# Two passes instead of three for the gate and up products of small experts

## The chip, the cores and the metric

The kernel runs on one NeuronCore of a Trainium2 chip. The metric is the device time of one execution in microseconds (us): the kernel before takes 2128.33 us, the median of three runs (2125.3 to 2130.84). Engines are named as in the profile: PE is TensorE (PEld its weight loads), DVE is VectorE, ACT is ScalarE, POOL is GpSimd and SP is the queue that issues loads.

## What is computed

Two transformer blocks on 512 tokens of width 1024, in float32. The part that matters here is the mixture of experts that ends the first block: 64 experts of hidden width 256, of which each token takes 8. Cut to this, the reference is:

```
out = swiglu(h_pad[tok], w_gu[e], w_down[e])      # silu(x @ gate) * (x @ up) @ down, for each expert e
acc = acc.at[tok].add(out * wts[:, None])         # its tokens only, weighted
```

`w_gu` is 1024 x 512 for each expert (gate and up side by side), `w_down` is 256 x 1024, so an expert has 3 MB of weights.

## The kernel before, in words

Products that have to keep float32 accuracy are made of three passes. Each operand is split into a high part (`hi`, rounded to the format `R` that PE takes in one pass) and a low part (`lo`, the rest): ACT writes `hi` by a copy, DVE writes `lo` by a subtraction. `mm3` (line 142) then adds high times high, high times low and low times high in PSUM.

The expert stage is the loop in `experts` (line 1256). Experts are ordered by how many tokens chose them, and the table `CAPS` gives each place in this order a fixed room: 3 experts with room for 192 tokens, 6 for 128, 21 for 96, 24 for 64 and 8 for 32, beside 2 fixed ones with 128. `plan` (line 1149) makes groups of them: two experts of 64 share one block of 128 rows (12 groups), a 96 and a 32 share one (8 groups), the other 13 experts of 96 and all of 128 have a block each, and an expert of 192 has a block of 128 and one of 64. This gives 44 groups, 47 blocks and 67 pairs of an expert and a block. The kinds of groups are mixed evenly over the stage.

For each block the rows are gathered by an indirect DMA (`xg`), turned by PE and split (`expert_rows`: tiles `xT`, tokens along the 128 columns that PE holds still). For each expert, its weights come in three loads of 1 MB (`raw`; gate and up two, down one), each split in two pieces (`split_unit`, lines 132 and 133: `whi` by ACT, `wlo` by DVE, 128 x 1024 each). `expert_in` (line 998) multiplies: the token block stands still, 512 columns of weights move past it, 8 steps of 128 along the width of 1024, three passes each, so 24 matmuls for each pair of an expert and a block, whatever the expert's room. `act` is silu of gate (ACT, line 1011) times up (DVE, line 1012). One group later `act` is turned and split (`expert_turn`), `expert_out` multiplies by down (12 matmuls), ACT scales the result into `ey`, and the result is added to the tokens in two ways: the first 384 columns by a product with a 0/1 matrix into PSUM (`expert_parts`, `expert_add`: tiles `eoh`, `eys`, `acc`), the others by an indirect DMA that adds in HBM (`expert_send`, tile `cb`, issued by POOL).

Each engine works through its own list in order. The lists are made by a scheduler when the program is built, from the order of the code and its own estimate of times; buffers decide the rest: five `raw` tiles, eight pieces of `whi` and `wlo` each, four PSUM tiles `mm`. A load is issued when DVE has split the tile that it overwrites. Behind the loop a branch (line 1312) skips a loop for experts with more tokens than their room.

Of the kernel before, what the change touches and what calls it, by code (L numbers as in the profile page):

```python
# [21 lines left out]
T = 512  # L22
# [43 lines left out]
class Kernel:  # L66
# [918 lines left out]
    def expert_rows(self, tiles, pp, xg, m=128):  # L985

        nc = self.nc
        pool, tags = tiles
        xT = [pool.tile([128, KD, 128], R, tag=tag, name="xT", bufs=2)[:, :, 0:m] for tag in tags]
        for u in range(2):  # L990
            p2 = pp.tile([128, 4, 128], F, tag="mm", name="tp", bufs=4)[:, :, 0:m]
            for k in range(4):
                c = (4 * u + k) * 128
                nc.tensor.transpose(p2[:, k], xg[0:m, c:c + 128], self.ident[0:m, 0:m])
            self.split_ps(xT[0][:, 4 * u:4 * u + 4], xT[1][:, 4 * u:4 * u + 4], p2)
        return xT

    def expert_in(self, pp, gu, blocks, between=None):

        nc = self.nc  # L1000
        pss = [pp.tile([128, 512], F, tag="mm", name="mm", bufs=4) for _ in blocks]
        for u in range(2):
            w = self.split_unit(gu[u].rearrange("p (k n) -> p k n", k=4), 4, 512)
            for ps, (xT, *_) in zip(pss, blocks):
                for k in range(4):
                    kk = 4 * u + k
                    self.mm3(ps[0:xT[0].shape[2]], [z[:, kk] for z in xT], [z[:, k] for z in w], kk == 0, kk == KD - 1)
            if u == 0 and between:
                between()
        for ps, (xT, a, p0, p1) in zip(pss, blocks):  # L1010
            nc.scalar.activation(a[p0:p1], ps[p0:p1, 0:256], AF.Silu)
            nc.vector.tensor_mul(a[p0:p1], a[p0:p1], ps[p0:p1, 256:512])  # L1012

    def expert_turn(self, mp, pp, a):

# [27 lines left out]
    def expert_parts(self, mp, y, row, bufs=2):  # L1043

        nc = self.nc
        m = row.shape[0]
        yh, yl = (mp.tile([128, CA], R, tag=f"eys{i}", name="eys", bufs=bufs)[0:m] for i in range(2))
        nc.scalar.activation(yh, y[0:m, :CA], AF.Copy)  # L1048
        last = nc.gpsimd.tensor_sub(yl, y[0:m, :CA], yh.bitcast(F))  # L1049
        oh = mp.tile([128, T], R, tag="eoh", name="eoh", bufs=bufs)[0:m]  # L1050
# [119 lines left out]
    def experts(self, mp, pp, h2d, cb, acc, shared, gT, sums, grow, ahead, extra):  # L1170
# [42 lines left out]
        def turn(g):  # L1213

            if g < len(groups):
                xT[g] = []
                for b in groups[g][1]:
                    free.append(xg_of[count[1]])
                    xT[g].append(self.expert_rows(tiles, pp, free[-1], b[-1][2]))
# [23 lines left out]
        sums()  # L1243
        n = len(xgs)
        more = grow()
        tiles = more, ("xT0", "xT1")
        room(mp, AHEAD2)
        free.extend(xgs[n:])
        for _ in range(AHEAD2):
# [6 lines left out]
        for g in range(len(groups) + 1):  # L1256
# [36 lines left out]
            if g < len(groups):  # L1293
                es, bs = groups[g]
                a = [mp.tile([128, 256], F, tag="eact", name="act", bufs=4)[0:b[-1][2]] for b in bs]
                now = g, a, []
                for j, e in enumerate(es):
                    e = number(e)
                    now[2].append(e)
                    self.expert_in(pp, gu(e), [(xT[g][b], a[b], p0, p1) for b, parts in enumerate(bs)  # L1300
                                               for i, p0, p1, _ in parts if i == j], None if j else advance)
                    finish()
            else:
                advance()
# [4 lines left out]
        ahead()  # L1309
        xp = extra.enter_context(tc.tile_pool(name="extra", bufs=1))  # L1310
        total = self.further(xp)
        with tc.If(total > 0):
            cnt = xp.tile([128, 1], F, name="xcnt")
            nc.vector.memset(cnt, 0.0)
            with tc.For_i(0, total):
                pos, aux, e = self.extra_block(xp, cnt)
                row, wt, gi, _ = self.slot_tables(xp, pp, [[(pos, aux, 0, 128, 0)]])[0]
                ev = nc.sync.value_load(e[0:1, 0:1], min_val=0, max_val=63)
                self.gather(gi, xgs[0], h2d)
                a = mp.tile([128, 256], F, tag="eact", name="act", bufs=4)  # L1320
                self.expert_in(pp, gu(ev), [(self.expert_rows(tiles, pp, xgs[0]), a, 0, 128)])
                y = mp.tile([128, D], F, tag="ey", name="ey", bufs=2)
                self.expert_out(pp, dn(ev), [(self.expert_turn(more, pp, a), wt, y, 0, 128)])
                self.expert_add(acc, *self.expert_parts(xp, y, row, 1)[0])
# [635 lines left out]
```

## Time and profile before

| what | value |
|---|---|
| median of three runs | 2128.33 us |
| the profiled execution: its own time | 2128.15 us |
| the profiled execution: span from first to last instruction | 2126.4 us |
| PE busy over the span | 2038.1 us (96%) |
| DVE busy over the span | 1425.5 us (67%) |
| ACT busy over the span | 1090.8 us (51%) |
| POOL busy over the span | 486.2 us (23%) |
| moved by DMA | 386.68 MB, mean 182 GB/s |

The shares are means over stages that differ. The expert stage, from the first gate product at 585.7 us to the last down product at 1282.7 us, is a third of the span; its own rows stand in the section below. A busy time in a row of a window counts a moment once, however many instructions overlap in it; a group's mean is the length of one instruction, which on DVE and PE can overlap the next.

### The profile page before, as it was taken

What the parts mean: (1) busy time and instruction counts of PE and PEld (TensorE: products, weight loads), DVE (VectorE), ACT (ScalarE), POOL (GpSimd) and SP (SyncE); (2) the same over time, 40 slices, a digit from 0 to 9 for tenths busy, and PEclk for the clock granted to TensorE, in tenths of its full rate; (3) what the DMA queues carried; (4) which work ended last, traced back from release to release, by engine and by line L of the source; (5) the groups of instructions that cost most, each with busy time, mean ns of one, the idle gap of its engine ahead of it and who ended that gap; (6) DMA issues with size and microseconds to landing.
All of it is one profiled execution on the core that took longest, in us unless ns stands there. A gap on an engine that the chain in (4) does not pass through costs nothing. (4 is left out here: it accounts for less than half of the span.)

```text
span 2126.4 us, 28083 instructions
## 1 busy us (share of the span) xinstructions
PE 2038.1 (96%) x10311; PEld 1663.4 (78%) x10311; DVE 1425.5 (67%) x2444; ACT 1090.8 (51%) x1569; POOL 486.2 (23%) x307
## 2 busy tenths in 40 slices
PE   7999999999899999999999996999999999999998
PEld 4777888877787788877887784877788878888886
DVE  6667767647899799989999785455853345333344
ACT  7445443233387788878887884334232224232232
POOL 0322231011144343524334213011100001010110
PEclk9999999999899999999999998999999999999999
DMA  7211136633499899999999885312122333222221
GB/s 297 70 41 48 53 111 261 235 110 147 177 322 335 290 341 352 339 325 307 337 336 337 289 290 188 132 60 70 50 89 79 114 115 116 92 100 99 99 80 40
DMA packets 69713, 386.68 MB, mean 182 GB/s; under 512 B 11374, under 2 KB 12351, under 8 KB 30020
## 3 DMA queue, kind: packets, MB, share of 16 engines
q1 hardware_dynamic: 56932, 357.56, 45.6%
q0 software_dynamic: 12640, 27.29, 5.5%
q8 instruction: 82, 1.34, 0.2%
q14 instruction: 59, 0.48, 0.1%
HBM read 369.99 MB, written 23.55 MB: 185 GB/s over the span
## 5 line engine op out<-in xcount | busy, mean ns | idle before, releaser
L133 DVE TENSOR_TENSOR wlo<-raw,whi 128x1024 fp32r<-128x1024 f32 x586 | 728.0, 1258 | 252.0 <-ACT whi L132 244.0
L132 ACT ACTIVATE whi<-raw 128x1024 fp32r<-128x1024 f32 x592 | 621.0, 1057 | 385.6 <-PE mm L147 190.7
L146 PE MATMUL mm<-whi,xT 128*128 128x512 f32 (+2 forms) x536 | 219.7, 410 | 0.1
L147 PE MATMUL mm<-wlo,xT 128*128 128x512 f32 (+2 forms) x536 | 211.9, 395 | 0.0
L148 PE MATMUL mm<-whi,xT 128*128 128x512 f32 (+2 forms) x536 | 211.9, 395 | 0.0
L1039 POOL DMA_INDIRECT cb<-ey,sgi x67 | 130.9, 1954 | 233.4 <-ACT ey L1035 148.4
L146 PE MATMUL mm<-hT,whi 128*128 128x512 f32 x320 | 127.0, 397 | 0.0
L147 PE MATMUL mm<-hT,whi 128*128 128x512 f32 x320 | 125.8, 394 | 0.0
L148 PE MATMUL mm<-hT,wlo 128*128 128x512 f32 x320 | 125.5, 392 | 0.0
L147 PE MATMUL mm<-x,whi 128*128 128x512 f32 x304 | 122.5, 403 | 0.0
L148 PE MATMUL mm<-x,wlo 128*128 128x512 f32 x304 | 120.8, 398 | 0.0
L146 PE MATMUL mm<-x,whi 128*128 128x512 f32 x304 | 120.8, 397 | 0.0
L148 PEld LDWEIGHTS mm<-whi,xT 128*128 128x128 f32 (+2 forms) x536 | 96.8, 181 | 27.8
L146 PEld LDWEIGHTS mm<-whi,xT 128*128 128x128 f32 (+2 forms) x536 | 97.2, 181 | 23.1 <-DVE act L1012 0.5
L1565 POOL TENSOR_TENSOR relu<-relu 128x512 f32<-128x512 f32 x32 | 42.9, 1341 | 315.0 <-ACT relu L1563 315.0
L147 PEld LDWEIGHTS mm<-wlo,xT 128*128 128x128 f32 (+2 forms) x536 | 97.2, 181 | 22.3
L1049 POOL TENSOR_TENSOR eys<-ey,eys 128x384 fp32r<-128x384 f32 (+2 forms) x47 | 79.2, 1686 | 141.2 <-ACT eys L1048 114.3
L148 PE MATMUL mm<-whi,eaT 128*128 128x512 f32 (+2 forms) x268 | 105.8, 396 | 0.4 <-DVE eaT L153 0.2
L147 PE MATMUL mm<-wlo,eaT 128*128 128x512 f32 (+2 forms) x268 | 105.8, 395 | 0.0
L146 PE MATMUL mm<-whi,eaT 128*128 128x512 f32 (+2 forms) x268 | 105.8, 395 | 0.0
L146 PE MATMUL mm<-y,whi 128*128 128x512 f32 (+2 forms) x272 | 103.2, 380 | 0.0
L148 PE MATMUL mm<-y,wlo 128*128 128x512 f32 (+2 forms) x272 | 103.1, 379 | 0.0
(534 smaller groups left out, 4488.9 us busy)
## 6 DMA issues: line engine op xcount, KB each, us to landing
raw<-in_w_expert_gu SPq DMA_DIRECT2D x128, 1024.0 KB
raw<-in_w_expert_down SPq DMA_DIRECT2D x64, 1024.0 KB
raw<-in_w_in SPq DMA_DIRECT2D x41, 1024.0 KB
raw<-in_w_ff SPq DMA_DIRECT2D x32, 1024.0 KB
raw<-in_w_ada SPq DMA_DIRECT2D x24, 1024.0 KB
raw<-in_w_out SPq DMA_DIRECT2D x8, 1024.0 KB
raw<-in_w_v SPq DMA_DIRECT2D x4, 1024.0 KB
raw<-in_w_ret_up SPq DMA_DIRECT2D x4, 1024.0 KB
```

Source lines behind the costliest of these rows:

```text
L132: nc.scalar.activation(hi, rv[:, k:k + n], AF.Copy)
L133: (engine or nc.vector).tensor_sub(lo, rv[:, k:k + n], hi.bitcast(F))
L146: mm(ps, ah, bh, start=start, stop=False)
L147: mm(ps, ah, bl, start=False, stop=False)
L148: mm(ps, al, bh, start=False, stop=stop)
L1039: self.nc.gpsimd.indirect_dma_start(out=cb, out_offset=bass.IndirectOffsetOnAxis(ap=gi, axis=0), in_=y[p0:p1, CA:], in_offset=None, bounds ...
L1049: last = nc.gpsimd.tensor_sub(yl, y[0:m, :CA], yh.bitcast(F))
L1565: nc.gpsimd.tensor_mul(sq, r, r)
```

## The change

For an expert with room for up to 64 tokens the high and the low part of its rows are put side by side in the 128 columns that PE holds still. One pass over `whi` and one over `wlo` then give both parts' products: rows 0 to n of PSUM hold the high part's, rows n to 2n the low part's (n tokens). Their sum is the result; it holds low times low too, which three passes leave out. So 16 matmuls take the place of 24 for each such pair of an expert and a block. In exchange ACT copies the second half of the rows out of PSUM (`esum`, n x 512), DVE adds the first half to it, and silu and product then read `esum` from SBUF. The pairs concerned are the 24 experts of 64, the 8 of 32 and the second blocks of the 3 experts of 192: 35 of 67.

`expert_rows` writes the parts where they are wanted: for two experts of 64 in one block by one copy and one subtraction of the same size as before with other strides, for a 96 beside a 32 by two of each (96 and 32 tokens wide). The tile `xT` holds both parts in one tile of the size of the two before. Apart from this, `add()` moves ahead of the branch, and the loop behind it uses other buffers; the trace shows no instruction of that loop.

```
     def expert_in(self, mp, pp, gu, blocks, between=None):
...
+                    if len(xT) == 2:
+                        self.mm3(ps[0:xT[0].shape[2]], [z[:, kk] for z in xT], [z[:, k] for z in w],
+                                 kk == 0, kk == KD - 1)
+                    else:
+                        for i, z in enumerate(w):
+                            nc.tensor.matmul(ps[0:xT[0].shape[2]], xT[0][:, kk], z[:, k],
+                                             start=kk == i == 0, stop=kk == KD - 1 and i == 1)
...
+            if len(xT) == 2:
+                nc.scalar.activation(a[p0:p1], ps[p0:p1, 0:256], AF.Silu)
+                nc.vector.tensor_mul(a[p0:p1], a[p0:p1], ps[p0:p1, 256:512])
+            else:
+                n = p1 - p0
+                s = mp.tile([128, 512], F, tag="esum", name="esum", bufs=2)[p0:p1]
+                nc.scalar.activation(s, ps[n:2 * n], AF.Copy)
+                nc.vector.tensor_add(s, ps[0:n], s)
+                nc.scalar.activation(a[p0:p1], s[:, 0:256], AF.Silu)
+                nc.vector.tensor_mul(a[p0:p1], a[p0:p1], s[:, 256:512])
...
     def expert_rows(self, tiles, pp, xg, parts=((0, 128),)):
...
+            elif w == 64:
+                v = x.rearrange("p k (j h w) -> p k h j w", j=2, h=2)
+                cut = [(lambda z: z.rearrange("p k (j w) -> p k j w", j=2), v[:, :, 0], v[:, :, 1])]
+                out = [(x[:, :, 0:128],), (x[:, :, 128:256],)]
+            else:
+                cut = [(lambda z: z[:, :, 0:w], x[:, :, 0:w], x[:, :, 256 - w:256]),
+                       (lambda z: z[:, :, w:m], x[:, :, w:m], x[:, :, m:256 - w])]
+                out = [(x[:, :, 0:w], x[:, :, 256 - w:256]), (x[:, :, w:256 - w],)]
...
+            for some, hi, lo in cut:
+                self.split_ps(hi[:, 4 * u:4 * u + 4], lo[:, 4 * u:4 * u + 4], some(p2))
...
         total = self.further(xp)
+        add()
         with tc.If(total > 0):
...
-        add()
```

How the lists change is shown at the second expert of the first group of two with room for 64. On PE, before, the last step's matmuls of its gate and up product (`mm_5781` is the PSUM tile, `whi_5810` and `wlo_5811` are the last piece of its weights, `xT_5469` and `xT_5470` the high and low part of the rows) stand so:

```order
L146 MATMUL mm_5781<-whi_5810,xT_5469 128x512
L147 MATMUL mm_5781<-wlo_5811,xT_5469 128x512
L148 MATMUL mm_5781<-whi_5810,xT_5470 128x512
L146 MATMUL mm_5781<-whi_5810,xT_5469 128x512
L147 MATMUL mm_5781<-wlo_5811,xT_5469 128x512
L148 MATMUL mm_5781<-whi_5810,xT_5470 128x512
```

And of the change, for the same expert (`mm_5776`, last piece `whi_5801` and `wlo_5802`):

```order
L1033 MATMUL mm_5776<-whi_5801,xT_5467 128x512
L1033 MATMUL mm_5776<-wlo_5802,xT_5467 128x512
L1033 MATMUL mm_5776<-whi_5801,xT_5467 128x512
L1033 MATMUL mm_5776<-wlo_5802,xT_5467 128x512
```

Six matmuls for a piece have become four; both parts of the rows are one operand. On DVE, before, the same expert's last weight piece and its product `act` stand so:

```order
L133 TENSOR_TENSOR wlo_5811<-raw_5804,whi_5810 128x1024
L133 TENSOR_TENSOR wlo_5861<-raw_5858,whi_5860 128x1024
L133 TENSOR_TENSOR wlo_5865<-raw_5858,whi_5864 128x1024
L133 TENSOR_TENSOR wlo_5891<-raw_5888,whi_5890 128x1024
L133 TENSOR_TENSOR wlo_5895<-raw_5888,whi_5894 128x1024
L1051 TENSOR_SCALAR eoh_6035<-riota_3961,srow_5058 128x512
L133 TENSOR_TENSOR wlo_5915<-raw_5912,whi_5914 128x1024
L133 TENSOR_TENSOR wlo_5919<-raw_5912,whi_5918 128x1024
L903 TENSOR_TENSOR oh_6057<-riota_3961,rpos_3974 128x4x96
L133 TENSOR_TENSOR wlo_5954<-raw_5951,whi_5953 128x1024
L1012 TENSOR_TENSOR act_5664<-act_5664,mm_5781 64x256
```

And of the change, from the same expert's last piece to its sum and product:

```order
L133 TENSOR_TENSOR wlo_5802<-raw_5795,whi_5801 128x1024
L133 TENSOR_TENSOR wlo_5850<-raw_5847,whi_5849 128x1024
L133 TENSOR_TENSOR wlo_5854<-raw_5847,whi_5853 128x1024
L133 TENSOR_TENSOR wlo_5880<-raw_5877,whi_5879 128x1024
L133 TENSOR_TENSOR wlo_5884<-raw_5877,whi_5883 128x1024
L1046 TENSOR_TENSOR esum_5813<-mm_5776,esum_5813 64x512
L153 TENSOR_TENSOR xT_5818<-tp_5819,xT_5818 128x4x128
L153 TENSOR_TENSOR xT_5818<-tp_5826,xT_5818 128x4x128
L1048 TENSOR_TENSOR act_5664<-act_5664,esum_5813 64x256
```

The result of PE is now awaited four pieces after the last one that PE needs for it, where it was seven; over the whole stage DVE's sums stand 2.9 pieces behind on the mean, where its products stood 6.6 behind. The same moves on ACT: where one silu stood, a copy and a silu stand, with other work of ACT between them:

```order
L1045 ACTIVATE esum<-mm 64x512
L152 ACTIVATE xT<-tp 128x4x128 x2
L132 ACTIVATE whi<-raw 128x1024
L1047 ACTIVATE act<-esum 64x256
L132 ACTIVATE whi<-raw 128x1024 x2
```

Here the copy of the same expert is followed by the two halves of the next block's rows and a weight piece before its silu, so the wait for DVE's sum has work in front of it.

## Rows read from the trace of the kernel before

**Rows 1.** busy time by engine: the expert stage and three stretches in it

```profile
core 0: us, PE busy (x) PEld busy (x) DVE busy (x) ACT busy (x) POOL busy (x), PEclk, DMA share, GB/s
585.70:1282.70 697.00, 692.35 (x3522) 551.62 (x3521) 625.51 (x912) 576.61 (x767) 271.40 (x155) 1.00 0.92 323
600.00:700.00 100.00, 97.68 (x524) 78.16 (x523) 96.36 (x168) 81.63 (x109) 49.98 (x24) 1.00 0.94 332
698.30:738.00 39.70, 39.60 (x200) 30.30 (x198) 28.78 (x33) 29.44 (x43) 13.04 (x8) 1.00 0.86 291
796.00:812.20 16.20, 16.20 (x81) 13.11 (x79) 16.20 (x19) 13.32 (x18) 9.37 (x4) 1.00 1.00 355
```

**Rows 2.** groups by line, expert stage: busy us, mean ns | idle us before, releasers

```profile
L133 DVE TENSOR_TENSOR wlo<-raw,whi 128x1024 fp32r<-128x1024 f32 x383 | 471.6, 1252 | 58.2 <-ACT whi L132 53.9
L132 ACT ACTIVATE whi<-raw 128x1024 fp32r<-128x1024 f32 x382 | 401.6, 1057 | 77.4 <-PE mm L148 74.0 <-DVE wlo L133 0.7 <-DVE srow L915 0.3
L146 PE MATMUL mm<-whi,xT 128*128 128x512 f32 (+2 forms) x536 | 219.7, 410 | 0.1
```

**Rows 3.** waits of the expert stage: us in total, times, longest us

```profile
ACT whi L132 <- PE mm L148: 74.0, 140, 5.5
DVE wlo L133 <- ACT whi L132: 53.9, 83, 3.6
POOL cb L1039 <- DMA cb<-ey,sgi: 40.9, 12, 8.1
...
SPq L118 <- DVE wlo L133: 469.0, 159, 14.1
```

**Rows 4.** timeline of PE: start us, length us; four products of one expert

```profile
1159.49 0.40 PE L146 MATMUL mm<-whi,xT 128*128 128x512 f32 x1
...
1160.19 0.40 PE L146 MATMUL mm<-whi,xT 128*128 128x512 f32 x1
```

**Rows 5.** timeline of DVE, weight splits back to back

```profile
657.31 2.35 DVE L133 TENSOR_TENSOR wlo<-raw,whi 128x1024 fp32r<-128x1024 f32 x2
659.58 0.41 DVE L1012 TENSOR_TENSOR act<-act,mm 128x256 f32<-128x256 f32 x1
659.91 4.65 DVE L133 TENSOR_TENSOR wlo<-raw,whi 128x1024 fp32r<-128x1024 f32 x4
```

**Rows 6.** nearest operations on DVE and ACT, by form, whole run

```profile
L1731 DVE TENSOR_TENSOR rb<-mm,rtab x8: 692/693/694, 1417.4 to 1490.3; 64x512 f32<-64x512 f32 x8
...
L153 DVE TENSOR_TENSOR xT<-tp,xT 128x512 fp32r<-128x512 f32 x62 | 39.9, 680 | 3.7 <-ACT xT L152 3.4
...
L153 DVE TENSOR_TENSOR xT<-tp,xT 128x384 fp32r<-128x384 f32 x26 | 13.2, 550 | 1.0 <-ACT xT L152 0.7
...
L153 DVE TENSOR_TENSOR cT<-hm,cT 128x256 fp32r<-128x256 f32 x8 | 3.3, 412 | 0.0
...
L153 DVE TENSOR_TENSOR eaT<-tp,eaT 128x128 fp32r<-128x128 f32 x3 | 0.8, 277 | 0.0
...
L152 ACT ACTIVATE xT<-tp 128x512 fp32r<-128x512 f32 x62 | 33.8, 594 | 17.7 <-PE tp L994 12.7 <-PE mm L147 4.5
...
L152 ACT ACTIVATE xT<-tp 128x384 fp32r<-128x384 f32 x26 | 11.3, 487 | 0.2
```

**Rows 7.** windows (columns of Rows 1) and timeline of PE: clock at the stage start

```profile
574.90:588.50 13.60, 9.00 (x71) 8.04 (x72) 12.34 (x52) 2.39 (x4) 4.69 (x5) 0.50 0.79 294
...
576.22 0.41 PE L908 MATMUL tp<-raux,oh 128*96 128x6 bf16 x4 [3.23 <-DVE raux L808]
...
586.70 0.63 PE L148 MATMUL mm<-whi,xT 128*128 128x512 f32 x1
587.12 0.63 PE L146 MATMUL mm<-whi,xT 128*128 128x512 f32 x1
```

**Rows 8.** DMA issues of the expert stage: count and us to landing

```profile
cb<-ey,sgi POOLq DMA_INDIRECT x66, 7.0
```

**Rows 9.** timeline of PE behind the last expert

```profile
1284.10 1.78 PE L1058 MATMUL acc<-eys,eoh 96*128 96x384 f32 x8
```

More of the change, by code (lines that the diff above doesn't have):

```diff
@@ L983, in gather, with expert_rows @@
                                           bounds_check=T - 1, oob_is_err=False)
-    def expert_rows(self, tiles, pp, xg, m=128):
+    def expert_rows(self, tiles, pp, xg, parts=((0, 128),)):
         nc = self.nc
         pool, tags = tiles
-        xT = [pool.tile([128, KD, 128], R, tag=tag, name="xT", bufs=2)[:, :, 0:m] for tag in tags]
+        m = parts[-1][1]
+        w = parts[0][1]
+        if len(tags) == 2:
+            hi, lo = (pool.tile([128, KD, 128], R, tag=tag, name="xT", bufs=2)[:, :, 0:m] for tag in tags)
+            cut, out = [(lambda z: z, hi, lo)], [(hi, lo)]
+        else:
+            x = pool.tile([128, KD, 256], R, tag=tags[0], name="xT", bufs=2)
+            if len(parts) == 1:
+                at = 128 if w > 64 else w
+                hi, lo = x[:, :, 0:w], x[:, :, at:at + w]
+                cut, out = [(lambda z: z, hi, lo)], [(hi, lo) if w > 64 else (x[:, :, 0:2 * w],)]
+            elif w == 64:
[6 more added lines that the diff above has]
+                out = [(x[:, :, 0:w], x[:, :, 256 - w:256]), (x[:, :, w:256 - w],)]
         for u in range(2):
@@ L994, in expert_rows, with expert_in @@
                 nc.tensor.transpose(p2[:, k], xg[0:m, c:c + 128], self.ident[0:m, 0:m])
-            self.split_ps(xT[0][:, 4 * u:4 * u + 4], xT[1][:, 4 * u:4 * u + 4], p2)
-        return xT
-    def expert_in(self, pp, gu, blocks, between=None):
+            for some, hi, lo in cut:
+                self.split_ps(hi[:, 4 * u:4 * u + 4], lo[:, 4 * u:4 * u + 4], some(p2))
+        return out
+    def expert_in(self, mp, pp, gu, blocks, between=None):
         nc = self.nc
@@ L1006, in expert_in @@
                     kk = 4 * u + k
-                    self.mm3(ps[0:xT[0].shape[2]], [z[:, kk] for z in xT], [z[:, k] for z in w], kk == 0, kk == KD - 1)
+                    if len(xT) == 2:
[5 more added lines that the diff above has]
+                                             start=kk == i == 0, stop=kk == KD - 1 and i == 1)
             if u == 0 and between:
@@ L1041, in expert_send, with expert_parts @@
                                           compute_op=OP.add)
-    def expert_parts(self, mp, y, row, bufs=2):
+    def expert_parts(self, mp, y, row):
         nc = self.nc
         m = row.shape[0]
-        yh, yl = (mp.tile([128, CA], R, tag=f"eys{i}", name="eys", bufs=bufs)[0:m] for i in range(2))
+        yh, yl = (mp.tile([128, CA], R, tag=f"eys{i}", name="eys", bufs=2)[0:m] for i in range(2))
         nc.scalar.activation(yh, y[0:m, :CA], AF.Copy)
         last = nc.gpsimd.tensor_sub(yl, y[0:m, :CA], yh.bitcast(F))
-        oh = mp.tile([128, T], R, tag="eoh", name="eoh", bufs=bufs)[0:m]
+        oh = mp.tile([128, T], R, tag="eoh", name="eoh", bufs=2)[0:m]
         nc.vector.tensor_scalar(oh, self.route["iota"][0:m], row, None, op0=OP.is_equal)
@@ L1218, in turn @@
                     free.append(xg_of[count[1]])
-                    xT[g].append(self.expert_rows(tiles, pp, free[-1], b[-1][2]))
+                    xT[g].append(self.expert_rows(tiles, pp, free[-1], [p[1:3] for p in b]))
                     rows_of.setdefault(g, []).append(count[1])
@@ L1245, in experts @@
         more = grow()
-        tiles = more, ("xT0", "xT1")
+        tiles = more, ("xT",)
         room(mp, AHEAD2)
@@ L1299, in experts @@
                     now[2].append(e)
-                    self.expert_in(pp, gu(e), [(xT[g][b], a[b], p0, p1) for b, parts in enumerate(bs)
-                                               for i, p0, p1, _ in parts if i == j], None if j else advance)
+                    self.expert_in(mp, pp, gu(e), [(xT[g][b][i], a[b], p0, p1) for b, parts in enumerate(bs)
+                                                   for i, (k, p0, p1, _) in enumerate(parts) if k == j],
+                                   None if j else advance)
                     finish()
```

7 lines of the change are left out of this document (3 added, 4 removed).

## The prediction, made before the changed kernel ran

> **What bounds the kernel now.** I read the page first: PE is busy for 96% of the span. Such a share can't say what PE time is worth in one stage, so I cut out the expert stage, from the first gate product to the last down product, and asked for busy time by engine [rows 1]. In its 697.0 us PE is busy for 692.35, DVE for 625.51 (89.7%), ACT for 576.61; the DMA share is 0.92, about 641 us of transfers. So PE sets the pace, and three others follow within 10 to 17%. Inside the stage the picture changes with the kind of group: in the 16.2 us around one group of two 64s, DVE and PE are both full; from 698.3 to 738.0 us, with an expert of 192, DVE rests for 10.9 of 39.7 us.
>
> Next, the waits [rows 2, 3]. DVE's idle time stands in front of the weight splits and waits for ACT (53.9 us); ACT's waits for PE (74.0 us), that is for PE to let go of a `whi` piece. This is back-pressure from PE: DVE and ACT have split all the pieces there is room for. SP's loads wait for DVE to finish with a `raw` tile (469.0 us), and no wait for a weight load is among the long ones. The reader is to see a line of engines held up from its far end, PE; taking work from PE speeds the stage up until the next engine, DVE, is full.
>
> **What the change removes and adds.** PE: 35 pairs of an expert and a block go from 24 to 16 matmuls, 280 fewer. Three successive ones start 0.70 us apart [rows 4], 0.233 each (the length of 0.40 counts the overlap), so PE loses 65.3 us and has 692.4 - 65.3 = 627 left.
>
> DVE: 35 sums of n x 512. The nearest row is a product of 64 x 512 from PSUM and SBUF that also moves 64 partitions, 0.693 us [rows 6]; in a full list an operation starts about 0.08 us before the last ends (0.41 long, 0.33 to the next start [rows 5]), so 0.61 is the lower bound: 21 to 24 us, and I take 23. The product afterwards reads SBUF alone: 0.412 for 256 columns from SBUF [rows 6] against 0.41 now [rows 5], nothing. In the 8 blocks of a 96 and a 32, 16 subtractions of 512 columns (0.680) become one of 384 (0.550) and one of 128 (0.277) [rows 6]: 16 x 0.147 = 2.4 us. The strided subtractions for two 64s have the same number of elements; I take them at the same time, for want of a row with these strides; the bound above is 24 x 0.68 us more if they took twice as long, 16 us. DVE: 625.5 + 25.4 = 651.
>
> ACT: 35 copies at 0.594 [rows 6], 21 us, and 16 times one more narrow copy, at most 0.487 + 0.487 - 0.594 = 0.38 each, 6 us: 604 at most. With the stage at 675 it is still the emptiest of the three; a copy that stands ahead of a weight piece delays DVE only when ACT has no lead left. DMA moves the same bytes. `add()` ahead of the branch moves eight products (1.78 us [rows 9]) that ran back to back with their neighbours: between nothing and 1.8 us, I take nothing. The loop behind the branch doesn't run. SP's and POOL's lists keep their instructions.
>
> **The sum.** The full engine is now DVE with 651 us of work. How well can it be filled? Two rows bound it: for 16.2 us it reaches 100%, which would make the stage 651 (46 us shorter); over the 100 us from 600 to 700, where PE and DVE both have over 96%, it reaches 96.4% [rows 1]. That stretch is the nearest to the new state, with two engines almost full that wait for each other in turn, so I take 0.964: 651 / 0.964 = 675, 22 us shorter. The experts of 96, 128 and 192 keep PE as their slowest engine and the pairs get DVE; the eight pieces of `whi` and `wlo` let DVE work ahead by 8 x 1.14 us [rows 5], 9 us, which carries a pair's extra through the neighbouring group. Of the 65 us taken from PE a third arrives. The profiled execution took 2128.15 us, 0.2 below the median, so 2128.2 - 22 = 2106.
>
> **What could be late next.** The lists were made anew. DVE's sum stands fewer pieces behind the matmuls that it needs than the product did, four instead of seven at the place shown. Behind a waiting sum stand the weight splits, and for these PE waits, so a late sum costs DVE time that isn't made good. Four pieces last 4.6 us [rows 5] and PE needs 0.9 us for a piece's four matmuls; for ACT's copy 0.6 is to be added. So the places with two pieces (2.3 us) just hold.
>
> **Rivals.**
> (a) DVE is the bound and the stage takes 661 to 693 us, as above: 2092 to 2124. Chance 0.62.
> (b) The new lists fill DVE to over 98.5%, as the stretch of 16.2 us shows to be possible: 651 to 661, 2082 to 2092. Against it stands that the stretch is short. Chance 0.12.
> (c) The transfers become the bound. For: a share of 0.92, at times 1.00 [rows 1]. Against: loads wait for DVE, not DVE for loads [rows 3]. If the share can't pass 0.95, the stage takes 641 / 0.95 = 675, if not 0.93, 689: 2106 to 2120, and weight copies on ACT would wait for `raw`. Chance 0.08.
> (d) Nothing arrives: the sums and the copies wait for PE in lists with less lead, and DVE idles for 40 to 52 us of the stage: 691 to 703, within 6 us of before. Chance 0.10.
> (e) Slower: the same mechanism, worse. It decides from 46 us of idle time (697 - 651). If DVE kept the 71.5 us that it idles now, the stage would take 722 and the kernel 2153. Against: that idle time is PE's back-pressure, which the change takes away. Chance 0.05.
> (f) The clock. [...] Chance 0.03.
> [...]
> POOL's adds into `cb` land 7.0 us after their issue [rows 8] and wait for one another (40.9 us [rows 3]); with the one behind the stage, 67 x 7.0 = 469 us is far below 675, so I give that no case of its own.
>
> **How the numbers follow.** The time is that of (a) at 0.964. Two in ten are left out of 2088 to 2122: most of (b), (e), (f), and parts of (d). A change of 0.3%, 6 us, is about what the runs of before can tell from none (2125.3 to 2130.84). Faster by more, below 2122: (a) but for its last 2 us, (b) and (c), 0.81. Within: (d) and that rest, 0.12. Slower: (e), (f), 0.07.
>
> **What would show it.** Right: 280 fewer matmuls at the same 0.23 us; sums of 0.61 to 0.69 us; PE with gaps of its own, waiting for `wlo`; DVE at 95 to 98% in a stage of 661 to 693 us; the rest of the span unchanged to a few us. Wrong: sums or strided subtractions that take much longer; DVE below 94% with waits for ACT's copies; ACT waiting for loads; a granted clock below 1.00 in the stage.

## The result, and the profile after

| | before | after |
|---|---|---|
| median of 5 runs, us | 2125.89 | 2146.27 |
| lowest to highest, us | 2125.3 to 2130.84 | 2140.62 to 2152.75 |
| ratio | | 1.0093, 95% interval 1.0068 to 1.0119 |
| profiled execution: time, span, us | 2128.15, 2126.4 | 2145.43, 2143.7 |
| expert stage, us | 697.0 | 712.9 |

The kernel became 20 us slower. The forecast was 2106 us and faster: wrong in sign, and outside the range. Outside the stage nothing happened: 2143.7 - 712.9 = 1430.8 us now, 2126.4 - 697.0 = 1429.4 before. The windows of the profile after (columns as in [rows 1]): the stage and two bad stretches in it.

```profile
586.60:1299.50 712.90, 656.16 (x3243) 497.03 (x3242) 638.35 (x960) 576.76 (x815) 320.59 (x155) 0.97 0.89 313
856.00:884.00 28.00, 19.95 (x88) 15.63 (x87) 19.18 (x23) 15.43 (x22) 12.66 (x4) 0.88 0.79 268
1020.00:1040.00 20.00, 14.74 (x61) 11.89 (x60) 11.34 (x28) 9.89 (x16) 7.68 (x5) 0.83 0.78 247
```

PE now rests for 712.90 - 656.16 = 56.7 us (4.65 before), as intended. But DVE rests for 74.6 us (71.5 before [rows 1]): it is 89.5% full, not 96.4%. POOL is busy 49 us longer with the same work (320.59 against 271.40), and the granted clock is below 1.00. Next the groups by line of the stage (busy us, mean ns | idle before, releasers):

```profile
L133 DVE TENSOR_TENSOR wlo<-raw,whi 128x1024 fp32r<-128x1024 f32 x379 | 457.5, 1245 | 20.6 <-ACT whi L132 19.6
...
L1075 POOL DMA_INDIRECT cb<-ey,sgi x66 | 163.0, 2470 | 253.5 <-ACT ey L1071 112.6 <-DMA cb<-ey,sgi 71.2 <-DVE wlo L133 24.7
L1033 PE MATMUL mm<-wlo,xT 128*128 128x512 f32 (+1 forms) x280 | 115.8, 414 | 4.2 <-DVE wlo L133 4.1
L1033 PE MATMUL mm<-whi,xT 128*128 128x512 f32 (+1 forms) x280 | 114.4, 409 | 1.9 <-ACT whi L132 1.6 <-ACT ey L1071 0.4
...
L1046 DVE TENSOR_TENSOR esum<-mm,esum 64x512 f32<-64x512 f32 (+1 forms) x35 | 23.8, 681 | 13.3 <-ACT esum L1045 12.7
L1045 ACT ACTIVATE esum<-mm 64x512 f32<-64x512 f32 (+1 forms) x35 | 20.8, 593 | 23.2 <-PE mm L1033 22.6
```

The new operations cost what was forecast. DVE's wait for `whi` fell from 53.9 us [rows 2] to 19.6. What is new is POOL's send: 2.47 us in the mean, 1.96 before (129.5 us for 66). The waits of the stage (us in total, times, longest) show who suffers:

```profile
POOL cb L1075 <- DMA cb<-ey,sgi: 71.2, 17, 8.8
...
PE acc L1094 <- POOL eys L1085: 25.5, 14, 8.1
...
ACT esum L1045 <- PE mm L1033: 22.6, 14, 10.3
ACT ey L1071 <- DMA cb<-ey,sgi: 19.9, 6, 6.8
DVE wlo L133 <- ACT whi L132: 19.6, 20, 6.1
...
DVE xT L153 <- ACT xT L152: 14.2, 12, 6.2
...
DVE esum L1046 <- ACT esum L1045: 12.7, 10, 8.2
DVE eaT L153 <- ACT eaT L152: 11.1, 11, 5.4
...
PE mm L146 <- DVE esum L1046: 5.1, 1, 5.1
```

Before, PE waited 1.4 us for `eys`, and ACT 2.0 us for a send to let go of `ey`. One wait of PE for `eys` in the timeline (start us, length us):

```profile
860.05 9.18 POOL L1075 DMA_INDIRECT cb<-ey,sgi  x1 [4.69 <-DVE eoh L1087]
...
861.12 6.89 DVE L133 TENSOR_TENSOR wlo<-raw,whi 128x1024 fp32r<-128x1024 f32 x6
...
869.54 1.01 POOL L981 DMA_INDIRECT xg<-h2d,sgi  x1 [0.30 <-issue]
870.57 1.01 POOL L1085 TENSOR_TENSOR eys<-ey,eys 96x384 fp32r<-96x384 f32 x1
...
871.63 1.01 PE L1094 MATMUL acc<-eys,eoh 96*128 96x384 f32 x2 [8.05 <-POOL eys L1085]
...
872.44 0.63 PE L1033 MATMUL mm<-wlo,xT 128*128 128x512 f32 x1
...
872.87 0.63 PE L1033 MATMUL mm<-whi,xT 128*128 128x512 f32 x1
...
875.54 0.59 ACT L1045 ACTIVATE esum<-mm 64x512 f32<-64x512 f32 x1 [10.25 <-PE mm L1033]
```

A send lasts 9.18 us, over a run of DVE's weight splits without a pause, and ends about 1 us behind it. Only then come a gather and `eys`; PE has stood 8.05 us at the `acc` products, which the new list puts right behind their own group; its next products start 0.43 us apart, at a granted clock of 0.50 (867.90 to 874.73 us); ACT's copy for the sum has waited 10.25 us. In the stage 24 of POOL's sends, gathers and `eys` last over 3 us (9 before), and each of the 24 lies over weight splits. Taking its length alone off its end shows where each got in: 11 at the end of a run of splits, 8 at an instruction of DVE with an input in PSUM (`esum`, `xT`, an `act` with three passes) and 5 at the comparison `eoh`.

That POOL is late is one half; the other is the order of PE's list. Counted in the traces, the `acc` products of 9 of the 47 blocks stand before any down product of the next group in the kernel before, and of 25 in the kernel after. The others stand 2 to 24 down products further back and leave POOL that lead. The account of the lists ahead of the prediction doesn't look at this place.

POOL's sends hurt in a second way: ACT waits 19.9 us until a send lets go of `ey`. The one long wait of PE for a sum comes behind such a wait:

```profile
731.41 0.68 ACT L1071 ACTIVATE ey<-mm,swt 64x512 f32<-64x512 f32 x1 [6.82 <-DMA cb<-ey,sgi]
...
741.07 0.74 PE L146 MATMUL mm<-whi,xT 128*96 128x512 f32 x1 [5.08 <-DVE esum L1046]
```

### The profile page after: what moved, and what is told of

Read it like the earlier page. It is cut to its first block, busy times and chain, and to the rows that moved or that the text cites. A ratio compares the mean times of both kernels' runs of the same rounds, so it can differ in the third digit from the quotient of the medians.

```text
span 2143.7 us, 27459 instructions
## 1 busy us (share of the span) xinstructions
PE 2003.4 (93%) x10031; PEld 1610.5 (75%) x10031; DVE 1444.8 (67%) x2495; ACT 1094.4 (51%) x1620; POOL 538.4 (25%) x307
## 5 line engine op out<-in xcount | busy, mean ns | idle before, releaser
L133 DVE TENSOR_TENSOR wlo<-raw,whi 128x1024 fp32r<-128x1024 f32 x586 | 720.2, 1256 | 216.0 <-ACT whi L132 211.4
L132 ACT ACTIVATE whi<-raw 128x1024 fp32r<-128x1024 f32 x592 | 607.3, 1055 | 331.3 <-PE mm L147 191.7
L1075 POOL DMA_INDIRECT cb<-ey,sgi x67 | 165.2, 2466 | 257.3 <-ACT ey L1071 112.6
L1033 PE MATMUL mm<-wlo,xT 128*128 128x512 f32 (+1 forms) x280 | 115.8, 414 | 4.2 <-DVE wlo L133 4.1
L1033 PE MATMUL mm<-whi,xT 128*128 128x512 f32 (+1 forms) x280 | 114.4, 409 | 1.9 <-ACT whi L132 1.6
L1094 PE MATMUL acc<-eys,eoh 128*128 128x384 f32 (+2 forms) x376 | 88.3, 357 | 28.6 <-POOL eys L1085 26.9
L146 PE MATMUL mm<-whi,xT 128*96 128x512 f32 (+1 forms) x256 | 107.3, 419 | 5.3 <-DVE esum L1046 5.1
L147 PE MATMUL mm<-wlo,xT 128*96 128x512 f32 (+1 forms) x256 | 104.2, 407 | 3.5 <-DVE wlo L133 3.4
L981 POOL DMA_INDIRECT xg<-h2d,sgi x47 | 87.6, 1864 | 76.9 <-issue 26.2
L1071 ACT ACTIVATE ey<-mm,swt 64x512 f32<-64x512 f32 (+3 forms) x134 | 88.5, 680 | 34.4 <-DMA cb<-ey,sgi 19.9
```

What stands on the lines that cost most here:

```text
L132: nc.scalar.activation(hi, rv[:, k:k + n], AF.Copy)
L133: (engine or nc.vector).tensor_sub(lo, rv[:, k:k + n], hi.bitcast(F))
L146: mm(ps, ah, bh, start=start, stop=False)
L147: mm(ps, ah, bl, start=False, stop=False)
L981: self.nc.gpsimd.indirect_dma_start(out=xg[0:gi.shape[0]], out_offset=None, in_=h2d, in_offset=bass.IndirectOffsetOnAxis(ap=gi, axis=0), b ...
L1033: nc.tensor.matmul(ps[0:xT[0].shape[2]], xT[0][:, kk], z[:, k], start=kk == i == 0, stop=kk == KD - 1 and i == 1)
```

## The experiments

Three theories were tested. *GpSimd theory*: POOL is shut out by DVE's unbroken splits, and PE, which has lost its surplus, waits for it. *Chain theory*: the sums come late through PE, ACT, DVE. *Ring or full-engine theory*: with PE, DVE and ACT all nearly full each delay is passed on, and DVE can't be filled to 96% at all. The table has one row for a kernel. Each ratio is to the kernel before run beside it (medians 2125.89 to 2129.35 us), so ratios compare two kernels better than their times do. DVE share is its busy time over the stage. "Gaps" are PE's idle times over 1 us, summed; "slow" the products that started while the granted clock was 0.50 (3 to 7 of them stand at the stage's start); the last column is PE's wait of `acc` for POOL's `eys`.

| kernel | median us (runs) | ratio to before, 95% | stage us | DVE share | gaps us | slow | eys us |
|---|---|---|---|---|---|---|---|
| before | 2125.89 (5) | 1 | 697.0 | 89.7% | 0.0 | 7 | 1.4 |
| after | 2146.27 (5) | 1.0093, 1.0068 to 1.0119 | 712.9 | 89.5% | 39.0 | 91 | 25.5 |
| e1_yl_on_dve | 2133.92 (10) | 1.0024, 1.0002 to 1.0046 | 703.8 | 90.5% | 28.3 | 70 | - |
| e2_no_sums | 2110.11 (4) | 0.9912, 0.9879 to 0.9944 | 676.0 | 90.7% | 16.6 | 62 | 13.8 |
| e3_sums_alone | 2141.78 (4) | 1.0052, 1.0036 to 1.0069 | 709.2 | 91.2% | 3.8 | 45 | 2.6 |
| e4_acc_later | 2134.42 (10) | 1.0026, 1.0012 to 1.0040 | 700.0 | 91.6% | 33.9 | 144 | 0 |
| e5_no_sums_acc_later | 2107.28 (4) | 0.9896, 0.9875 to 0.9918 | 676.4 | 91.1% | 15.8 | 82 | 3.1 |
| e6_only_32s | 2116.83 (4) | 0.9939, 0.9921 to 0.9957 | 688.1 | 91.5% | 5.6 | 38 | 3.8 |
| e7_only_64s | 2114.16 (4) | 0.9933, 0.9911 to 0.9955 | 680.0 | 92.5% | 13.0 | 50 | 8.8 |
| e10_64s_acc_later | 2123.78 (10) | 0.9983, 0.9973 to 0.9992 | 691.5 | 92.8% | 18.6 | 78 | 0 |
| e11_32s_acc_later | 2123.70 (10) | 0.9986, 0.9977 to 0.9996 | 696.7 | 90.4% | 13.2 | 65 | 0 |
| e12_64s_more_sums | 2134.69 (5) | 1.0033, 0.9993 to 1.0072 | 702.9 | 90.4% | 27.0 | 90 | 18.8 |

**Where PE meets POOL.** e1 takes `eys` from POOL (and, with it, no longer holds a group's sends behind `eys`); e4 holds the `acc` products behind the next group's last down product.

```diff
 # e1, in expert_parts
-        last = nc.gpsimd.tensor_sub(yl, y[0:m, :CA], yh.bitcast(F))
+        nc.vector.tensor_sub(yl, y[0:m, :CA], yh.bitcast(F))
...
-        return (oh, (yh, yl)), last
+        return (oh, (yh, yl)), None
 # e4, in finish; end is the last product of expert_out
-                    add()
+                    with tc.issue_after(end.ins):
+                        add()
```

> The changed kernel, with the low part of eys (384 columns, 47 times in the stage) subtracted by VectorE instead of GpSimd. Nothing is left out. GpSimd theory (its instructions stand still while VectorE splits weights without a pause, and TensorE then waits for eys): TensorE's wait of acc for eys, 25.5 us in the stage, falls below 8 us, though VectorE has some 47 x 0.5 = 24 us more to do; 2120 to 2145. Chain theory (the sums come too late, TensorE to ScalarE to VectorE, and VectorE idles for them): that wait is not what costs; VectorE's extra 24 us come on top, 2155 to 2175.

> The changed kernel, with the products into acc held behind the last down product of the following group, where the code has them, instead of directly behind their own group. Nothing is left out. GpSimd theory: GpSimd is as late as before (its sends still 2.3 us or more in the mean), but TensorE has a group's lead on it: the wait of acc for eys falls from 25.5 us to below 6, most falls of the clock go, 2105 to 2128. Chain theory: the sums are as late as they were, 2138 to 2155.

Both take the wait away, and both gain 12 us by the times, 14 to 15 by the ratios; their intervals don't overlap with that of after. So PE's wait for POOL costs some 12 to 15 us of the 20, as far as two edits can tell that also make the lists anew. e1 changes one more thing: no split of DVE lasts over 1.4 us there, where 14 do in after, some 11 us beyond their 1.23. The wait isn't all: both kernels are still slower than before, and e4's 2134 lies between what the GpSimd theory (up to 2128) and the chain theory (from 2138) allowed. e1 leaves ACT's wait for the sends as it was (23.9 us), in e4 it is 6.1. e4's waits now stand in many places of a few us each:

```profile
DVE wlo L133 <- ACT whi L132: 23.3, 34, 1.7
ACT eaT L152 <- PE tp L1056: 17.6, 10, 5.6
...
PE tp L1056 <- DVE act L1048: 9.3, 9, 2.5
...
PE tp L908 <- DVE xT L153: 7.8, 3, 3.1
...
PE tp L1014 <- DVE xT L153: 6.6, 2, 4.2
```

**The two parts of the change alone.** e2 drops the copy and the addition (so the low part of the rows is left out of gate and up); e3 is the kernel before, with sums of zeros put in; e5 is e2 with e4's edit.

```diff
 # e2, in expert_in of after
-                s = mp.tile([128, 512], F, tag="esum", name="esum", bufs=2)[p0:p1]
-                nc.scalar.activation(s, ps[n:2 * n], AF.Copy)
-                nc.vector.tensor_add(s, ps[0:n], s)
-                nc.scalar.activation(a[p0:p1], s[:, 0:256], AF.Silu)
-                nc.vector.tensor_mul(a[p0:p1], a[p0:p1], s[:, 256:512])
+                nc.scalar.activation(a[p0:p1], ps[0:n, 0:256], AF.Silu)
+                nc.vector.tensor_mul(a[p0:p1], a[p0:p1], ps[0:n, 256:512])
 # e3, in expert_in of before, for blocks of up to 64 tokens
...
+                nc.scalar.activation(s, ps[p0:p1], AF.Copy, scale=0.0)
+                nc.vector.tensor_add(s, ps[p0:p1], s)
...
```

> The changed kernel without the copies by ScalarE and the additions by VectorE: silu and product read the upper half of PSUM, so the low part of the rows is left out of gate and up. Two passes alone. Chain theory: with the chain gone the 65 us taken from TensorE arrive but for VectorE's bound of some 605 us at 0.96, stage about 640 to 660, 2070 to 2092. GpSimd theory: VectorE still splits weights without a pause and GpSimd is still held up; TensorE's waits for eys stay above 10 us, stage 670 to 695, 2100 to 2125.

> The kernel before (three passes) with the sums alone: ScalarE writes 512 columns of zeros times PSUM, VectorE adds them to PSUM, silu and product read the sum; the result stays the same, and 35 copies and 35 additions are added. Chain theory: late sums delay the weight splits behind them, +10 to +25 us, 2136 to 2151. GpSimd theory: TensorE stays the bound with 692 us, VectorE keeps its pauses for ScalarE and GpSimd gets through; within 6 us of before, 2120 to 2132, GpSimd's sends under 2.1 us in the mean.

> The two passes alone of e2_no_sums (the low part of the rows is left out of gate and up) with the products into acc held a group later as in e4_acc_later. If GpSimd's lateness is all that keeps e2 from the time of its fullest engine, TensorE's 13.8 us of waiting for eys go and the stage falls from 676 to about 660: 2085 to 2095. If TensorE, VectorE and ScalarE, all with little to spare, wait for one another in a ring, other waits grow in their place, as in e4, where 25 us of waiting went and 12 us were gained: 2096 to 2108.

Two passes alone bring 19 us (e2), or 22 (e5); the sums alone cost 12 where PE is the full engine (e3: more than the GpSimd theory allowed, and what the chain theory said). With e4's order the sums cost 2134.42 - 2107.28 = 27 us, for 24 us of work on DVE and 21 on ACT: with two passes DVE's work is passed on in full. e2 at 2110 refutes the chain theory's 2070 to 2092 for the kernel without sums, so late sums are a part of the loss and not the whole; e5 fell as the ring theory said.

**Which blocks.** e6 and e7 each keep three passes for the other sort of blocks (the rows' two parts are then laid out as before); e12 is e7 with e3's sums of zeros for the 32s and the second blocks of 192.

```diff
 # e6: the pairs of 64 as before; e7: the same for w == 32 and for a 192's second block
-                out = [(x[:, :, 0:128],), (x[:, :, 128:256],)]
+                hi, lo = x[:, :, 0:128], x[:, :, 128:256]
+                cut, out = [(lambda z: z, hi, lo)], [(hi, lo)] * 2
```

> The changed kernel with two passes for the 8 experts of 32 beside a 96 and the 3 second blocks of 192 alone; the 24 experts of 64 keep three passes: 88 matmuls fewer (20 us) and 11 sums. GpSimd and ring theory: these blocks stand where TensorE is the slowest engine, VectorE keeps its pauses elsewhere, the clock stays at full: faster, 2108 to 2122. Chain theory (a sum costs what it delays, 20 us for 35): 11 of them, 2130 to 2138.

> The complement: two passes for the 24 experts of 64 in pairs alone, three for the 32s and the second blocks of 192: 192 matmuls fewer (45 us) and 24 sums. GpSimd and ring theory: the loss comes from these groups, where VectorE was already full and now splits without a pause: 2140 to 2160, GpSimd's sends at 2.2 us or more in the mean. Chain theory: 24 of 35 sums, 2136 to 2143. If both sorts of blocks are alike, e6 and e7 lie on a line between before and after.

> e7_only_64s (two passes for the 64s), where the 32s and the second blocks of 192 keep three passes but get a copy by ScalarE and an addition by VectorE as well (of zeros: the result stays): 7.5 us more for VectorE, 6.5 for ScalarE, nothing less for TensorE. Full-engine theory (with two passes for the 64s VectorE sets the pace, and each us more of it costs one or more): 2122 to 2135, which would also be why the whole change is so much slower than e7. Lead theory (it is the waits of these blocks in their order, above all their products with fewer matmuls, not VectorE's work): 2113 to 2120.

My expectation for e7 was a miss: each half of the change alone is faster than before, by 12 and by 15 us, and the two together 20 us slower. Mean us from a group's first gate product to the next group's, worked out from the traces (the last group, a 96, has no next and is left out):

| group (count) | before | e6 | e7 | after |
|---|---|---|---|---|
| two 64s (12) | 17.88 | 18.45 | 15.17 | 18.01 |
| a 96 and a 32 (8) | 18.35 | 16.84 | 18.95 | 17.91 |
| a 96 (12) | 13.98 | 14.01 | 14.94 | 14.97 |
| a 128 (6) | 12.90 | 12.97 | 12.78 | 14.38 |
| a 192 (3) | 18.27 | 16.80 | 18.39 | 16.77 |

In e7 the pairs of 64s give back 2.7 us each, the 96s take 1.0 and the pairs of a 96 and a 32 0.6. In after the pairs of 64s have lost all of it. e12 shows how little it takes: 7.5 us more for DVE put 20 us on e7, as the full-engine theory said. One mishap of its trace may be half of it: a gather of POOL that stood 9.90 us over eight splits, while PE waited 9.6. Its runs lie between 2120.74 and 2142.03. The order of PE's list goes along: the `acc` products stand before any down product of the next group in 10 blocks of e6, 14 of e7, 18 of e12, 20 of e2 and 25 of after, and PE's wait for `eys` is 3.8, 8.8, 18.8, 13.8 and 25.5 us.

> Two passes for the 24 experts of 64 alone (e7_only_64s), with the products into acc a group later (e4_acc_later). GpSimd theory: TensorE waits 8.8 us for eys in e7, which go: 2104 to 2111. Ring theory (what is taken from one wait turns up in another): 2111 to 2120. Nothing is left out.

> Two passes for the 32s and the second blocks of 192 alone (e6_only_32s), with the products into acc a group later. TensorE waits 3.8 us for eys in e6: 2111 to 2118 by either theory. Nothing is left out.

Two misses: e4's edit on e7 and on e6 takes the wait for `eys` away, and makes them 10 and 7 us slower (11 and 10 by the ratios). The lists are made anew each time, and another order of the same work is worth that much here; which part of the order, no run tells. It is nearly as much as e4 gained on after, so e4's gain can't be put down to the wait alone.

**What shuts POOL out.** Small programs by themselves: POOL's operations beside runs of DVE's subtractions of 128x1024.

> A small program by itself, which computes nothing of the reference (its output is ones and differences of them): GpSimd does six subtractions of 128x384, later four gathers, alone, and beside VectorE that does without a pause (1) 14 subtractions of 1024 columns from SBUF, (2) 56 of 256 columns, (3) 14 copies of 1024 columns with one input, (4) 24 subtractions of 512 columns with one input in PSUM. GpSimd theory: alone 1.0 to 1.5 us each; in (1) one GpSimd instruction lasts over several of VectorE's, 5 us or more, perhaps to the end of the run (16 us); in (3) and (4) no more than 2 us. Rival: GpSimd waits for no more than the one VectorE instruction under way, under 2.5 us each in every stretch, and the long ones in the kernel have another cause.

> Again a small program by itself, which computes nothing of the reference. In e8_lock VectorE's subtractions of 1024 columns wrote one tile and started 1.26 us apart with a length of 1.22, so one had ended before the next began, and GpSimd's got in between, one for one. In the kernel they start 1.13 us apart with a length of 1.21, so they overlap. Here GpSimd does six subtractions, later four gathers, beside 14 subtractions of VectorE that (1) write four tiles in turn, (2) read what an earlier one wrote, (3) write one float32 tile, as in e8, (4) wait for a ScalarE copy each. GpSimd theory, mended: where they overlap (1.13 us apart) GpSimd gets in nowhere and its first instruction lasts to the end of the run, 10 us or more; where they don't, 1.9 us. Rival: 1.9 us in all, the turns are fair however they follow, and the long ones in the kernel stay unexplained.

> A third small program by itself, which computes nothing of the reference. In e8 and e9 GpSimd's subtractions began before VectorE's run and took turns with it, 1.85 us each. In the kernel they join a run that is already going. Here each of GpSimd's instructions (a subtraction on 128 rows, one on 96, a gather of 128 rows, an adding send of 128x640) waits for the third of VectorE's 12 subtractions of 1024 columns and so joins the run in its middle; the run (1) goes without waits, (2) with each subtraction waiting for a ScalarE copy that is early, (3) as (1), with a write of one column after every second, (4) as (1), with a copy of one column after every second. GpSimd theory, mended again: who joins a going run gets no turn until it breaks: about 10 us in (1) and (2), at most 3.5 us in (3) or (4) or both. Rival: 2 us in all; then what holds GpSimd in the kernel isn't the run of VectorE as such.

The GpSimd theory as I had it fell three times. Alone a subtraction on POOL takes 0.99 us, beside DVE's 1.85 to 2.04, and DVE's takes 1.90 to 2.02 in place of 1.22: fair turns. Also for one that joins a run (timeline of e13):

```profile
21.56 8.83 DVE L64 TENSOR_TENSOR dc<-da,dh 128x1024 fp32r<-128x1024 f32 x7 [16.33 <-SPq L94]
25.20 1.84 POOL L71 TENSOR_TENSOR gc<-dc,ga 128x384 f32<-128x384 f32 x1 [22.64 <-DVE dc L64]
```

Beside DVE's copies with one input, or subtractions with one in PSUM, POOL took 1.32 and 0.99 us (e8). So I copied the pipeline itself:

> A fourth small program by itself, which computes nothing of the reference: the stage's pipeline in small. ScalarE copies a piece, VectorE subtracts it, TensorE reads both with four products, with six pieces in turn, and thereby with the kernel's waits; GpSimd's subtraction of 128x384 waits for a ScalarE copy, three times, and then its adding send, three times; all of it without and then with loads by SP at the same time. GpSimd theory: as in the kernel, some of GpSimd's last 4 us or more. Rival: at most 2.4 us, so that something else of the kernel must hold it.

```profile
18.51 25.06 DVE L47 TENSOR_TENSOR wlo<-raw,whi 128x1024 fp32r<-128x1024 f32 x22
...
20.99 25.34 POOL L54 TENSOR_TENSOR yl<-ey,yh 128x384 fp32r<-128x384 f32 x3 [20.03 <-ACT yh L53]
```

There it is, far stronger than in the kernel: three subtractions of 0.98 us take 25.34, the first of them 23.44, to the end of DVE's run of 22; a send took 23.29. Loads by SP changed nothing (25.33 and 23.70 us with them). e18 takes the pipeline apart, in seven stretches:

> A fifth small program by itself, which computes nothing of the reference. In e15 one subtraction of GpSimd lasted 23.4 us, to the end of VectorE's run, where each of VectorE's splits waits for a ScalarE copy and for TensorE; in e8, e9 and e13, with few such waits, GpSimd got its turn in 1.9 us. Here GpSimd does one subtraction in each of seven stretches of 22 splits: (1) as e15; (2) VectorE waits for ScalarE alone; (3) for TensorE alone; (4) to (7) as (1), with an instruction of VectorE in between: (4) a copy of 16 columns from SBUF after every second split, (5) a comparison of 512 columns with one SBUF input after every fourth, (6) a subtraction of 256 columns with an input in PSUM after every fourth, (7) one of 256 columns with two SBUF inputs after every fourth. If it is VectorE's waits that keep GpSimd out: 10 us or more in (1), and in (2), (3) or both; by what ended the holds in the kernel (eoh, esum and xT did, the product act and the 16 columns of e14 did not): under 6 us in (5) and (6), to the end of the run in (4) and (7). If it is something of TensorE's reading: (2) is short.

```profile
22.17 18.84 POOL L81 TENSOR_TENSOR yl<-ey,yh 128x384 fp32r<-128x384 f32 x1 [21.21 <-ACT yh L80]
49.35 18.83 POOL L81 TENSOR_TENSOR yl<-ey,yh 128x384 fp32r<-128x384 f32 x1 [8.33 <-ACT yh L80]
76.44 17.82 POOL L81 TENSOR_TENSOR yl<-ey,yh 128x384 fp32r<-128x384 f32 x1 [8.27 <-ACT yh L80]
102.60 3.20 POOL L81 TENSOR_TENSOR yl<-ey,yh 128x384 fp32r<-128x384 f32 x1 [8.34 <-ACT yh L80]
131.22 20.18 POOL L81 TENSOR_TENSOR yl<-ey,yh 128x384 fp32r<-128x384 f32 x1 [25.41 <-ACT yh L80]
159.74 3.28 POOL L81 TENSOR_TENSOR yl<-ey,yh 128x384 fp32r<-128x384 f32 x1 [8.34 <-ACT yh L80]
188.65 20.18 POOL L81 TENSOR_TENSOR yl<-ey,yh 128x384 fp32r<-128x384 f32 x1 [25.62 <-ACT yh L80]
```

POOL stays out to the end where DVE waits for ACT alone and where it waits for PE alone (2, 3). That the waits do it isn't shown: no stretch of e18 is without them, ACT copies beside the splits in all seven, and in stretch (4) of e9, where each subtraction waits for a copy of ACT as well, POOL kept its turns of 1.86 us. Stretch (2) of e13, where splits waited for ACT too and POOL got in after 1.85 us, settles nothing, since a copy of one column stands right behind the split on which POOL came:

```profile
83.35 1.85 POOL L71 TENSOR_TENSOR gc<-dc,ga 128x384 f32<-128x384 f32 x1 [12.50 <-DVE dc L64]
84.27 0.14 DVE L52 COPY z<-dh 128x1 f32<-128x1 f32 x1
```

With an instruction in between that has an input in PSUM, POOL got in (6, 3.28 us), as it did at `xT`, `esum` and `act` in the kernel (8 of the 24); with the comparison it didn't (5, 20.18 us) and with the copy of 16 columns it did (4, 3.20 us), both against my expectation. In e8 the two engines took turns (1.85 to 2.04 us); in e15 POOL stayed out over some twenty instructions of DVE (23.44 us), with a send too (23.29 us); why, no run shows.

**Breaks in the kernel.** e14 puts a copy of 16 columns behind every second split of after and holds the next split behind it, e17 a subtraction of 16 columns with two SBUF inputs, e16 the copy into e7.

```diff
-            (engine or nc.vector).tensor_sub(lo, rv[:, k:k + n], hi.bitcast(F))
+            with self.tc.issue_after(self.gap.ins) if self.gap else ExitStack():
+                last = (engine or nc.vector).tensor_sub(lo, rv[:, k:k + n], hi.bitcast(F))
+            if self.tick is not None and k:
+                with self.tc.issue_after(last.ins):
+                    self.gap = nc.vector.tensor_copy(self.tick, self.ones[:, 0:16])
```

> The changed kernel, with a copy of 128x16 (one SBUF input) by VectorE behind every second weight split of the stage, held in its place (192 copies of some 0.07 us, 13 us of VectorE). Nothing is left out. GpSimd theory: no run is longer than two splits, GpSimd's instructions get in: none over 4 us, sends at 2.0 us or less in the mean, TensorE's wait for eys below 10 us, 2125 to 2140 in spite of the 13 us. Rival (the runs don't hold GpSimd, as in the small programs): its long instructions stay, 2150 to 2165.

> The control to e14_breaks: the same places and nearly the same lists, but the small instruction is a subtraction of 128x16 with two SBUF inputs. GpSimd theory: it breaks nothing (in the kernel the product act, with two SBUF inputs, did not end a hold, eoh with one did), GpSimd's instructions of 4 to 9 us stay, 2150 to 2165. If any gap or any short instruction lets GpSimd in: as e14.

> Two passes for the 24 experts of 64 alone (e7_only_64s) with the copies of e14_breaks. GpSimd theory: TensorE's 8.8 us of waiting for eys go, VectorE has 13 us more to do: 2108 to 2118, as e7 or better. Rival: 13 us more for the fullest engine, 2122 to 2132.

All three were slower, beyond both ranges that I gave each: 2178.59 us (ratio 1.0238, 1.0221 to 1.0255), 2176.04 (1.0222, 1.0205 to 1.0239) and 2151.61 (1.0121, 1.0071 to 1.0171). The breaks break next to nothing in the kernel (timeline of e14):

```profile
693.63 5.95 POOL L1091 TENSOR_TENSOR eys<-ey,eys 96x384 fp32r<-96x384 f32 x1 [6.05 <-ACT eys L1090]
...
693.95 0.16 DVE L139 COPY tick<-ones 128x16 f32<-128x16 f32 x1
...
694.03 2.35 DVE L136 TENSOR_TENSOR wlo<-raw,whi 128x1024 fp32r<-128x1024 f32 x2
...
696.30 0.16 DVE L139 COPY tick<-ones 128x16 f32<-128x16 f32 x1
...
696.38 2.34 DVE L136 TENSOR_TENSOR wlo<-raw,whi 128x1024 fp32r<-128x1024 f32 x2
```

Counted in this trace, two of POOL's instructions over 3 us got in at such a copy, while 46 copies went by under them; 27 of POOL's instructions last over 4 us (19 in after). So e14, e16 and e17 test nothing of a kernel in which POOL gets in, and that one wasn't found. The breaks are 192 times 0.08 us of DVE, 15 us, and cost 32 us over after and 37 over e7. Not all of it is DVE's time: PE's wait for `eys` grew as well, from 25.5 us to 41.2 in e14 and 40.7 in e17, and from 8.8 to 23.2 in e16.

## Why the prediction was wrong, step by step

- **What the change removes: right.** 280 products fewer, at the same pitch. PE's busy time fell by 36 us only (656 us are left, where I had 627). 84 more products ran at a granted clock of 0.50, 40 of them of an expert's weights, 0.19 us dearer each, the others `acc` products and transposes at 0.16 and 0.10: some 13 us. The other 16 us, by difference, are products that stand alone and count with their whole length.
- **What it adds: right.** Sums 23.8 us (23 forecast), copies 20.8 (21), strided subtractions 0.68 us each, as taken. DVE's total in the stage is 638 us where I had 651: four splits that stood inside the stage now start behind its last down product (5 us), and a split takes 1.207 us of busy time (457.5 / 379) in place of 1.231, as more of them follow without a pause.
- **"How well can it be filled?": the step that failed.** I took 0.964 from 100 us of the kernel before in which PE and DVE were both full. Measured: 0.895. No kernel here filled DVE over a whole stage to more than 92.8%, and e4, with the whole change and no wait of PE for `eys`, reached 91.6%: 640.9 us in a stage of 700.0, three us more than before. My 651 over 0.92 to 0.93 is 700 to 708: no gain or a small loss, rival (d) and a little beyond. I held DVE's idle time to be back-pressure from PE that goes with the change. The back-pressure did go (DVE's wait for `whi` fell from 53.9 to 19.6 us), but waits behind ACT and PE came in its place: 14.2 us for `xT`, 12.7 for `esum`, 11.1 for `eaT`. A stretch picked because it is full leaves out what empties engines now and then; the kernel after has one too, 921.6 to 1021.6 us, with DVE at 97.9%. Before has no whole stage with DVE as its full engine (DVE's own share was 89.7%, behind PE), so a range down to 0.90 was to be kept open.
- **"POOL's adds ... no case of its own": failed too.** I asked whether POOL's sends add up to the stage (469 us against 675). The question was who waits for POOL, where PE's list has the `acc` products (25 blocks of 47 without a lead, 9 before), and whether what DVE does in its new lack of pauses can hold POOL up. By e1 and e4 that is worth 12 to 15 us, most of what takes the result from the same to slower.
- **Rival (e)** gives 2153 if DVE keeps the idle time of 71.5 us; it kept 74.6, and the time is 2146. Its mechanism, late sums, is shown only in part: the sums cost 12 us in e3, and PE waited for one once, 5.08 us; but ACT's longest wait for a sum's product, 10.25 us, stood behind POOL.
- **Rival (f)**, the clock: waits of PE of up to 8.05 us do occur, the granted clock falls to 0.50 in or behind them, seven times in the stage of after (as once before the first products of the stage in the kernel before [rows 7]), and 91 products run at that level. It makes each stall dearer (some 13 us in all), and each of the seven has a wait of PE of 1.4 us or more before it. The chance of 0.03 was my estimate and no run shows it; what the runs show is those 13 us, too little to undo the forecast's 22.

The stage's account, in us: -65.3 for 280 products, +39.0 for PE's gaps over 1 us, +13 for slow products, together -13; measured +15.9. The other 29 are PE's gaps below 1 us (17.8 us, 4.7 before) and products that stand alone (0.40 in place of 0.233; 16 us by difference). Open are what sets the 92%, why e4's order helps the whole change and hurts its halves, and what it is in DVE's runs of splits that keeps POOL out. The version to keep is e7, two passes for the experts of 64 alone: 2114.16 us, ratio 0.9933 (0.9911 to 0.9955), faster than both kernels; e6 (0.9921 to 0.9957) can't be told from it.

## What to carry to other kernels

When work goes from the full engine to one that has 10% left, take the fill of the new bound from a whole stage, not from its best stretch, and forecast each part of the change by itself: two halves that gain 12 and 15 us lost 20 together. Before an engine loses its pauses, look at the engines that work beside it: here GpSimd's sends went from 1.96 to 2.47 us in the mean while VectorE's wait for `whi` fell from 53.9 to 19.6 us, and the place of the `acc` products in TensorE's list was what hid it when GpSimd came late (TensorE waited 1.4 us for `eys` before, 25.5 after). When a scheduler makes the lists anew, compare the places of all products that wait for a slow engine, not only of those that the change is about. Price a wait from who stands behind it, not from the busy time of the engine that is waited for.

## What the runs showed of the hardware

- GpSimd's subtraction (0.99 us alone) took fair turns, 1.84 to 2.04 us, with the runs of VectorE's subtractions in e8, e9 and e13, and was kept out for 17.8 to 23.4 us, to the end of the run, in e15 and in five of the seven stretches of e18. VectorE's run had no pause meanwhile (1.13 us from start to start in e15). A send of GpSimd (1.55 us alone) was kept out for 23.3 us in e15; in e13 it took 2.32. What parts the two kinds of runs is open.
- In e18 GpSimd got in with an instruction of VectorE in between that has an input in PSUM (3.28 us); with a comparison of 512 columns or a subtraction of 256 columns from SBUF it did not (20.18 us each). With a copy of 16 columns it did in the small program (3.20 us) and in the kernel hardly ever (5.95 us over two of them in e14).
- TensorE's granted clock fell to 0.50 seven times in the stage of after, in or behind waits of 1.4 to 8.05 us; products of 512 columns then started 0.43 us apart in place of 0.233.
- Another order of nearly the same instructions, which is the scheduler's doing and not the chip's, was worth 7 to 12 us of 2125 (e4, e10, e11), more than most of the costs in the sum.
